# Where the remaining modulation sums are taken: first attention or merging stages

## The chip, the cores and the metric

One core of a Trainium2 chip. The metric is the time of one execution on the device in microseconds; a kernel is told by the median of its runs. Engines are named as the profile names them: PE is TensorE's matmul, PEld its weight load, DVE is VectorE, ACT ScalarE, POOL GpSimd and SP SyncE, which issues all the loads and stores of this kernel from one queue.

## What is computed

A backbone of two layers over 1024 latent tokens and 256 context tokens of 1024 channels. Each layer normalises its input and modulates it, runs three mixers beside each other (differential attention, a long convolution, a gated mixing of chunks), gates and projects each of them, merges the three by sigmoid gates, projects the result and adds it, gated, to its input. The modulation is a small product of a conditioning vector with a large matrix:

```python
def modulation(cond, w, b):
    m = jax.nn.silu(cond) @ w + b
    return jnp.split(m, 3, axis=-1)
...
        sh, sc, gt = modulation(c, ada_w[l], ada_b[l])
        shc, scc, gtc = modulation(c_ctx, ada_w[l], ada_b[l])
        h = rms_norm(x, norm_pre[l]) * (1.0 + sc[:, None]) + sh[:, None]
        hc = rms_norm(xc, norm_pre[l]) * (1.0 + scc) + shc
...
        x_new = x + gt[:, None] * rms_norm(out, norm_post[l])
```

There are two conditioning vectors, one for the latents (c) and one for the context (c_ctx), and the matrix of a layer has 1024 rows and 3072 columns, 24 blocks of 128.

## The kernel before, in words

Activations lie with 128 channels on the partitions and the tokens along the free dimension, in three chunks of 512, 512 and 256 tokens (the last is the context; layer 1 has only the first two in most places). Every dense product is three matmuls, on a rounded part (hh, wh) and what rounding left (hl, wl): mm3, lines 180 to 185. Weights come in blocks of 128 output channels through class Weights: SP loads a raw block wr (line 85, two buffers), ACT makes wh (line 103) and POOL, at some blocks DVE, makes wl (line 104), each with two buffers.

Stages follow each other: a first one with the filters and layer 0's first modulation part, and then in each layer phase_a (attention by heads, with blocks of the input projection as fill between its steps), phase_b (convolution and chunk mixing, with fill of the same kind), phase_m (merging) and phase_o or phase_last (output projection, with layer 0's also making layer 1's input).

The modulation has three uses in time. Layer 0's shift and scale (part 0) are needed at the very start and are made by matmuls (ada, line 247). Layer 0's gate (part 1) is needed in phase_o(0), layer 1's shift and scale at the end of phase_o(0), layer 1's gate in phase_last. These three are made by ada_rest (lines 275 to 297) on DVE: SP loads a piece aw of 128 rows by 256 of the 1024 columns of the transposed matrix (line 290, two buffers) and a piece acs of 256 columns of the two conditioning vectors, alike on every partition (line 286, one buffer, from csd); DVE multiplies them and sums over the columns with accum_out (line 293), once for each vector (for layer 1's gate once in all); four pieces make a row's sum, which a reduction joins (line 296). One step of this generator is one load of aw and its products. There are 32 steps for layer 0's gate, 64 for layer 1's shift and scale, and 32 for layer 1's gate. The scratch result at shares its two buffers (tag r2) with the rotary embedding of kvq (line 395), of which each head uses some before its sums.

In phase_a(0) the generator is laid beside the fill: after every second step of the fill one step of the sums (beside, line 157, used at line 570), and what is left after the four heads is drained (line 573). A head of layer 0 has 4 or 5 fill blocks of 12 steps.

phase_m (lines 1142 to 1189) goes over the three branches in the order 0, 2, 1. For each it loads the branch's output gy and its gate gg (lines 1159 and 1160), multiplies them (DVE and POOL by turns), and splits them into gh and gl. Then come 8 blocks of output channels: the sigmoid gates sel of the next block (gates, line 1195: computed from the input projection, evacuated by ACT at line 1201, or, if they were computed in an earlier stage, loaded and passed through ACT at lines 1208 and 1209), and the product pb of this block, multiplied by sel (line 1178 or 1180) and added into acc (line 1182, mostly POOL). In layer 0 the early gates are those of channels 2 to 7 of branches 2 and 1; branch 0's are all computed here. In branch 1 the sum is split at once into hh and hl for phase_o (line 1189).

The order on the engines is not simply that of the program's text. Tiles, buffers and semaphores are the framework's (TileContext): when the kernel is built, it lays out, engine by engine, the order in which instructions are handed to the queues; text that comes earlier has priority, and an instruction whose operands and buffer are reckoned to be there may go ahead of earlier text that has to wait. On the chip each engine takes its queue in that order.

Of the kernel before, what the change touches and what calls it, by code (L numbers as in the profile page):

```python
# [9 lines left out]
F32 = mybir.dt.float32  # L10
# [45 lines left out]
class Weights:  # L56
    """128-column blocks of weights in their order of use: loads and splits run ahead."""
# [13 lines left out]
    def again(self, i):  # L71
        """Whether use i is of the same block as the last but one use."""
        a, b = self.order[i - 2], self.order[i]
        return i > 1 and a[0] == b[0] == "out" and (a[1], a[3]) == (b[1], b[3])
# [65 lines left out]
def whole(x):  # L140
    """Block k of x [128, blocks, n], as pieces (columns, their source)."""
    return lambda k: [(slice(0, x.shape[2]), x[:, k, :])]
# [14 lines left out]
def beside(main, side):  # L157
    """main, with a step of side for every other step of it."""
    for i, w in enumerate(main):
        yield w  # L160
        if i % 2:
            next(side, None)


# [5 lines left out]
class Kernel:  # L170
# [16 lines left out]
    def rsqrt(self, out, x, t):  # L187
        """out = x ** -0.5 for x > 0, by Newton's steps from a guess of the exponent's bits."""
# [13 lines left out]
    def mean_rsqrt_steps(self, pool, psum, ss, n, width, tag="P"):  # L202
        """[128, n] of rsqrt(mean + eps), alike on every partition, from the [128, n] squares summed but
        for the sum over the partitions: the sums come as columns, the roots go out as rows."""
# [21 lines left out]
    def block(self, key, chunks, psum, evac, ahead=True):  # L226
        """One block of 128 output channels over the chunks of tokens; yields the weight of each step."""
# [19 lines left out]
    def ada(self, pool, psum):  # L247
        """Shift and scale of layer 0's modulation: rows of 256 channels, turned into columns."""
# [26 lines left out]
    def ada_rest(self, pool):  # L275
        """The other parts of the modulation, by sums over the free dimension."""
        nc = self.nc
        for l, part in ((0, 1), (1, 0), (1, 1)):
            b0, n = ((0, 16), (16, 8))[part]
            js = (0, 1) if (l, part) != (DEPTH - 1, 1) else (0,)  # L280
            sums = pool.tile([128, 16, 2, 4], F32, name="ams", tag="ams")
            ps = pool.tile([128, 16, 2], F32, name="amt", tag="amt")
            for i in range(4):
                s = slice(256 * i, 256 * i + 256)
                cs = pool.tile([128, 2, 256], F32, name="acs", tag="acs")
                nc.sync.dma_start(out=cs, in_=self.csd[:, :, s])
                for b in range(n):
                    w = pool.tile([128, 256], F32, name="aw", tag="aw", bufs=2)
                    t = pool.tile([128, 512], F32, name="at", tag="r2", bufs=2)[:, 0:256]
                    nc.sync.dma_start(out=w, in_=self.A["ada_wT"][l, b0 + b, :, s])  # L290
                    yield
                    for j in js:
                        nc.vector.scalar_tensor_tensor(out=t, in0=w, scalar=1.0, in1=cs[:, j, :], op0=MUL, op1=MUL,  # L293
                                                       accum_out=sums[:, b, j, i:i + 1])
            for j in range(2):
                nc.vector.reduce_sum(out=ps[:, 0:n, j], in_=sums[:, 0:n, j if j in js else 0, :], axis=AX.X)
            self.modulation(l, part, ps)
# [34 lines left out]
    def hnorm_steps(self, l, c, xt, r, pool, tag=None):  # L332
        """Normalised, modulated input of layer l for chunk c, split for the products."""
# [22 lines left out]
    def hmod(self, l, c, x):  # L356
        """As hnorm_steps, from the normalised input x [128, KT, n], in place."""
# [191 lines left out]
    def phase_a(self, l):  # L549
        nc = self.nc  # L550
        with ExitStack() as st:
# [8 lines left out]
            rest = self.ada_rest(P) if l == 0 else iter(())  # L560
            for h in range(HEADS):
# [8 lines left out]
                fill = beside(fill, rest)  # L570
                interleave(self.attn(l, h, P, psum), fill, 0.6 if l == 0 else 0.8)
                drain(fill)
            drain(rest)

# [1 line left out]
    # A sequence of 8 blocks of 128 is transformed at 2048 points: frequency p + 16 m comes from  # L576
    # A_p = sum_b u_b cos(pi p b / 8) and B_p = sum_b u_b sin(pi p b / 8), p = 0..8, through 128 x 128
    # matrices. Pair p holds (real | minus imaginary) of its 128 frequencies; p = 0 and p = 8 share one pair,
    # whose row 0 is (frequency 0 | frequency 1024), both real. Pairs 5, 6, 7 take -B_p and hold plus imaginary.
# [4 lines left out]
    def filter_hidden(self, l, P, psum):  # L584
        """Hidden features of the filters, [64, tokens], rounded over what rounding left; the context's apart."""
# [55 lines left out]
    def butterfly(self, U, P, ZW, pool_share):  # L641
        """U: [128, 10, w] with block b in slot SLOT[b]; yields a group's [(A, B), (A, B)]."""
# [52 lines left out]
    def transform(self, ps, p, pool, ra, rb, ia, ib):  # L695
        """Pair p into ps [128, 2, w]."""
# [9 lines left out]
    def back(self, ps, p, pool, y):  # L706
        """Pair p of products y [128, 2, 128] back to (A | B), [channels, 256]."""
# [1029 lines left out]
```

## Time and profile before

| | |
|---|---|
| median of 3 runs | 3242.26 us (3238.61 to 3243.84) |
| profiled execution, span from its first to its last instruction | 3238.8 us |
| profiled execution, own time | the page gives none beside the span |
| instructions | 43600 |
| TensorE's mean granted clock | 0.977 |

The median lies 3.5 us above the span of the profiled execution. A page of the profile is one execution: busy times of the engines, the span in slices, the transfers, the chain that ended last, and groups of instructions by line of the kernel. A group's line names the line of the kernel, the engine, the operation, what is written and read, the shapes and the count, then the busy time in us with the mean of one in ns, and the idle time of the engine just before such instructions with what ended most of it. Times within the span are counted from its start.

### The profile page before, as it was taken

The numbers are of one execution on the slowest core, as the hardware profiler recorded it, in microseconds if no ns is written. First come the engines' busy times: TensorE is split into PE (matmuls) and PEld (weight loads), VectorE is DVE, ScalarE is ACT, GpSimd is POOL, SyncE is SP. The second block draws the span as 40 slices with busy tenths as digits, with TensorE's granted clock in tenths as the row PEclk, the third lists the DMA queues.
The fourth block names the chain that finished last, engine by engine and source line by source line (L and its number), as shares of the span: only waits on it lengthen the run. The fifth ranks groups of instructions, "written<-read, shape, count | busy, mean of one in ns | idle before, by whom it ended". The sixth has DMA issues, their size and how long they took to land. (4 is left out here: it accounts for less than half of the span.)

```text
span 3238.8 us, 43600 instructions
## 1 busy us (share of the span) xinstructions
PE 3014.6 (93%) x16220; PEld 2529.3 (78%) x16220; DVE 1807.2 (56%) x3822; ACT 1219.6 (38%) x2015; POOL 958.5 (30%) x640
## 2 busy tenths in 40 slices
PE   8898999999989889999999899999998888899998
PEld 4687878788878777788877778888886767778878
DVE  6754767676875756202356745546456677432343
ACT  4322535353532423212344444545454233222231
POOL 1442020202023333212543322121214554321441
PEclk9899999999999999999999999999999999999999
DMA  6323222222356655413442421221214556542342
GB/s 240 111 85 107 76 72 77 78 76 77 109 187 200 196 162 184 142 40 99 130 159 86 156 64 49 66 60 60 62 61 156 188 178 192 169 156 80 112 134 79
DMA packets 234740, 381.62 MB, mean 118 GB/s; under 512 B 22622, under 2 KB 125406, under 8 KB 233248
## 3 DMA queue, kind: packets, MB, share of 16 engines
q1 hardware_dynamic: 234528, 378.83, 36.4%
q8 instruction: 128, 2.10, 0.3%
q14 instruction: 84, 0.69, 0.1%
HBM read 278.74 MB, written 90.57 MB: 114 GB/s over the span
## 5 line engine op out<-in xcount | busy, mean ns | idle before, releaser
L183 PE MATMUL pd<-hh,wh 128*128 128x512 f32 (+1 forms) x2784 | 1051.1, 378 | 11.0 <-DVE r L397 6.2
L185 PE MATMUL pd<-hh,wl 128*128 128x512 f32 (+1 forms) x2784 | 1037.4, 373 | 2.1 <-POOL wl L104 2.1
L184 PE MATMUL pd<-hl,wh 128*128 128x512 f32 (+1 forms) x2784 | 1038.1, 373 | 0.4 <-DVE hl L350 0.2
L104 POOL TENSOR_TENSOR wl<-wr,wh 128x1024 fp32r<-128x1024 f32 (+1 forms) x177 | 413.1, 2334 | 1416.3 <-ACT wh L103 1302.0
L183 PEld LDWEIGHTS pd<-hh,wh 128*128 128x128 f32 x2784 | 532.6, 191 | 93.0 <-DVE r L397 6.9
L185 PEld LDWEIGHTS pd<-hh,wl 128*128 128x128 f32 x2784 | 531.9, 191 | 87.0 <-POOL wl L104 2.5
L184 PEld LDWEIGHTS pd<-hl,wh 128*128 128x128 f32 x2784 | 532.6, 191 | 79.2 <-DVE hl L350 1.2
L103 ACT ACTIVATE wh<-wr 128x1024 fp32r<-128x1024 f32 (+1 forms) x204 | 194.9, 956 | 288.2 <-PE pd L184 135.4
L463 ACT ACTIVATE e<-S,sm 128x1280 f32<-128x1280 f32 (+1 forms) x144 | 177.7, 1234 | 203.9 <-DVE sm L461 184.8
L460 DVE TENSOR_REDUCE sm<-S 128x1 f32<-128x1280 f32 (+1 forms) x144 | 197.2, 1369 | 72.0 <-PE S L456 71.3
L183 PE MATMUL pb<-gh,wh 128*128 128x512 f32 (+1 forms) x480 | 178.4, 372 | 8.4 <-ACT gh L199 7.0
L185 PE MATMUL pb<-gh,wl 128*128 128x512 f32 (+1 forms) x480 | 178.3, 371 | 5.0 <-POOL wl L104 3.4
L184 PE MATMUL pb<-gl,wh 128*128 128x512 f32 (+1 forms) x480 | 178.5, 372 | 2.9 <-DVE gl L200 2.8
L456 PE MATMUL S<-K,q 128*128 128x512 f32 (+1 forms) x400 | 149.2, 373 | 13.9 <-ACT e L463 13.8
L293 DVE SCALAR_TENSOR_TENSOR at<-aw,acs 128x256 f32<-128x256 f32 x224 | 115.2, 538 | 47.3 <-DMA aw<-in_ada_wT 40.8
L456 PE MATMUL S<-K,w 128*128 128x512 f32 (+1 forms) x400 | 136.1, 354 | 0.0
L1178 DVE TENSOR_TENSOR acc<-pb,sel 128x512 f32<-128x512 f32 (+1 forms) x40 | 25.4, 637 | 189.7 <-PE pb L185 189.6
L200 DVE TENSOR_TENSOR pl<-T,ph 128x512 fp32r<-128x512 f32 x164 | 109.5, 686 | 33.2 <-ACT ph L199 31.6
L199 ACT ACTIVATE ph<-T 128x512 fp32r<-128x512 f32 x164 | 94.4, 596 | 73.7 <-PE T L493 73.6
L1182 POOL TENSOR_TENSOR acc<-acc,sel 128x512 f32<-128x512 f32 (+1 forms) x70 | 86.6, 1250 | 84.7 <-DVE sel L1180 84.6
L183 PEld LDWEIGHTS pb<-gh,wh 128*128 128x128 f32 x480 | 90.7, 189 | 26.8 <-ACT gh L199 8.6
L472 DVE SCALAR_TENSOR_TENSOR e<-e,sm,e 128x1280 f32<-128x1280 f32 (+1 forms) x72 | 104.7, 1455 | 10.5 <-ACT e L471 10.0
(405 smaller groups left out, 5228.0 us busy)
## 6 DMA issues: line engine op xcount, KB each, us to landing
wr<-in_w_in SPq DMA_DIRECT2D x136, 512.0 KB, 3.4
fm<-in_fmat SPq DMA_DIRECT2D x99, 192.0 KB, 3.1
fm<-in_imat SPq DMA_DIRECT2D x72, 256.0 KB, 3.0
aw<-in_ada_wT SPq DMA_DIRECT2D x128, 128.0 KB, 2.5
wr<-in_w_out SPq DMA_DIRECT2D x28, 512.0 KB, 3.4
zd<-zz SPq DMA_DIRECT2D x48, 256.0 KB, 2.0
z<-zd SPq DMA_DIRECT2D x24, 512.0 KB, 4.8
gd<-ev SPq DMA_DIRECT2D x48, 256.0 KB, 2.4
```

Source lines behind the costliest of these rows:

```text
L103: nc.scalar.activation(out=hi[:, 0:k, :], in_=t[:, 0:k, :], func=AF.Copy)
L104: eng.tensor_tensor(out=lo[:, 0:k, :], in0=t[:, 0:k, :], in1=hi[:, 0:k, :].bitcast(F32), op=SUB)
L183: mm(out, lhsT=wh, rhs=xh, start=first, stop=False)
L184: mm(out, lhsT=wh, rhs=xl, start=False, stop=False)
L185: mm(out, lhsT=wl, rhs=xh, start=False, stop=last)
L199: nc.scalar.activation(out=hi, in_=src, func=AF.Copy)
L200: nc.vector.tensor_tensor(out=lo, in0=src, in1=hi.bitcast(F32), op=SUB)
L293: nc.vector.scalar_tensor_tensor(out=t, in0=w, scalar=1.0, in1=cs[:, j, :], op0=MUL, op1=MUL, accum_out=sums[:, b, j, i:i + 1])
L456: nc.tensor.matmul(S[:, a - k0:b - k0], lhsT=st[:, o + 128 * t:o + 128 * t + 128], rhs=K[m][:, a:b], start=i == 0, stop=i == 1)
L460: nc.vector.reduce_max(out=sm[:, 0:1], in_=S[:, 0:nk], axis=AX.X)
L463: nc.scalar.activation(out=e[:, 0:nk], in_=S[:, 0:nk], func=AF.Exp, bias=sm[:, 1:2], scale=0.125, accum_out=sm[:, 2:3])
L472: nc.vector.scalar_tensor_tensor(out=e0[:, 0:nk], in0=e0[:, 0:nk], scalar=s0[:, 3:4], in1=e[:, 0:nk], op0=MUL, op1=ADD)
```

## The change

ada_rest takes the parts and the width of a piece as arguments. Layer 0's gate and layer 1's shift and scale are now summed in phase_m(0), in pieces of 128 columns; layer 1's gate in phase_m(1), in pieces of 256. The rows are taken in groups of 8 blocks, so that the partial sums are a smaller tile, and at gets a tag of its own with one buffer. In phase_m 9 steps in layer 0, and 2 in layer 1, follow each of the 24 blocks of products, and what is left is drained at the stage's end. beside and its use are gone. Steps: 64 + 128 in phase_m(0), 32 in phase_m(1). (Comments, which the change takes out too, are left out here.)

```diff
-def beside(main, side):
-    for i, w in enumerate(main):
-        yield w
-        if i % 2:
-            next(side, None)
...
-    def ada_rest(self, pool):
-        nc = self.nc
-        for l, part in ((0, 1), (1, 0), (1, 1)):
+    def ada_rest(self, pool, parts, w):
+        nc = self.nc
+        m = D // w
+        for l, part in parts:
             b0, n = ((0, 16), (16, 8))[part]
             js = (0, 1) if (l, part) != (DEPTH - 1, 1) else (0,)
-            sums = pool.tile([128, 16, 2, 4], F32, name="ams", tag="ams")
-            ps = pool.tile([128, 16, 2], F32, name="amt", tag="amt")
-            for i in range(4):
-                s = slice(256 * i, 256 * i + 256)
-                cs = pool.tile([128, 2, 256], F32, name="acs", tag="acs")
-                nc.sync.dma_start(out=cs, in_=self.csd[:, :, s])
-                for b in range(n):
-                    w = pool.tile([128, 256], F32, name="aw", tag="aw", bufs=2)
-                    t = pool.tile([128, 512], F32, name="at", tag="r2", bufs=2)[:, 0:256]
-                    nc.sync.dma_start(out=w, in_=self.A["ada_wT"][l, b0 + b, :, s])
-                    yield
-                    for j in js:
-                        nc.vector.scalar_tensor_tensor(out=t, in0=w, scalar=1.0, in1=cs[:, j, :], op0=MUL, op1=MUL,
-                                                       accum_out=sums[:, b, j, i:i + 1])
-            for j in range(2):
-                nc.vector.reduce_sum(out=ps[:, 0:n, j], in_=sums[:, 0:n, j if j in js else 0, :], axis=AX.X)
+            ps = pool.tile([128, n, 2], F32, name="amt", tag="amt")
+            for g in range(0, n, 8):
+                sums = pool.tile([128, 8, 2, m], F32, name="ams", tag="ams")
+                for i in range(m):
+                    s = slice(w * i, w * i + w)
+                    cs = pool.tile([128, 2, w], F32, name="acs", tag="acs")
+                    nc.sync.dma_start(out=cs, in_=self.csd[:, :, s])
+                    for b in range(8):
+                        a = pool.tile([128, w], F32, name="aw", tag="aw", bufs=2)
+                        t = pool.tile([128, w], F32, name="at", tag="at", bufs=1)
+                        nc.sync.dma_start(out=a, in_=self.A["ada_wT"][l, b0 + g + b, :, s])
+                        yield
+                        for j in js:
+                            nc.vector.scalar_tensor_tensor(out=t, in0=a, scalar=1.0, in1=cs[:, j, :], op0=MUL, op1=MUL,
+                                                           accum_out=sums[:, b, j, i:i + 1])
+                for j in range(2):
+                    nc.vector.reduce_sum(out=ps[:, g:g + 8, j], in_=sums[:, :, j if j in js else 0, :], axis=AX.X)
             self.modulation(l, part, ps)
...
-            rest = self.ada_rest(P) if l == 0 else iter(())
...
-                fill = beside(fill, rest)
                 interleave(self.attn(l, h, P, psum), fill, 0.6 if l == 0 else 0.8)
                 drain(fill)
-            drain(rest)
...
             ys = (self.ya[l], self.yd[l], self.yc[l])
+            rest = self.ada_rest(P, ((0, 1), (1, 0)), 128) if l == 0 else self.ada_rest(P, ((1, 1),), 256)
+            per = 9 if l == 0 else 2
...
                         if c == 0:
                             self.ws.ahead()
+                    for _ in range(per):
+                        next(rest, None)
                     if i == 1:
                         if d == 0:
                             self.mT = {c: self.alloc_h(c) for c in self.chunks(l)}
                         for c in self.chunks(l):
                             self.split(self.mT[c][0][:, d, :], self.mT[c][1][:, d, :], acc[c][:, d, :])
+            drain(rest)
```

## Rows read from the trace of the kernel before

**Rows 1.** The page, busy us of each engine over the span.

```profile
PE 3014.6 (93%) x16220; PEld 2529.3 (78%) x16220; DVE 1807.2 (56%) x3822; ACT 1219.6 (38%) x2015; POOL 958.5 (30%) x640
```

**Rows 2.** Stretches: length, busy us (PE, PEld, DVE, ACT, POOL), PEclk, DMA share, GB/s.

```profile
255.00:915.00 660.00, 626.58 (x3594) 535.06 (x3593) 446.12 (x1206) 297.33 (x481) 111.77 (x61) 0.99 0.27 85
1900.00:2400.00 500.00, 497.65 (x2691) 416.35 (x2690) 274.39 (x558) 247.45 (x367) 100.02 (x51) 1.00 0.18 59
1330.00:1676.00 346.00, 334.49 (x1717) 283.81 (x1716) 110.36 (x150) 91.62 (x166) 124.31 (x95) 0.99 0.35 106
2853.00:3126.00 273.00, 266.29 (x1151) 216.91 (x1150) 90.88 (x116) 74.46 (x118) 86.04 (x52) 0.99 0.36 114
```

**Rows 3.** The page's groups, the products of the sums.

```profile
L293 DVE SCALAR_TENSOR_TENSOR at<-aw,acs 128x256 f32<-128x256 f32 x224 | 115.2, 538 | 47.3 <-DMA aw<-in_ada_wT 40.8
```

**Rows 4.** Line 290, the loads of aw: issue on SP in ns, who waited, landing.

```profile
L290 SPq DMA_DIRECT2D aw<-in_ada_wT x128: 327/333/1944, 268.3 to 916.4; - x128
...
  DVE at L293: 40.8, 31
...
DMA to landing us min/median/max: 2.3/2.5/7.9
```

**Rows 5.** Stretches: the four bursts of sums within the first attention (columns as rows 2).

```profile
290.00:366.00 76.00, 70.86 (x384) 60.52 (x384) 53.35 (x153) 32.39 (x49) 12.18 (x7) 0.96 0.35 109
466.00:535.00 69.00, 62.52 (x348) 52.69 (x347) 50.63 (x150) 30.69 (x46) 7.39 (x3) 0.98 0.34 103
625.00:690.00 65.00, 61.80 (x352) 52.16 (x351) 49.39 (x150) 30.64 (x46) 7.38 (x3) 1.00 0.35 110
775.00:921.00 146.00, 138.22 (x805) 117.32 (x804) 109.76 (x333) 70.01 (x113) 17.36 (x8) 1.00 0.36 113
```

**Rows 6.** Waits of PE in 255 to 915 us: total, times, longest.

```profile
PE S L456 <- ACT e L463: 13.8, 5, 4.5
PE mrb L218 <- DVE mn L195: 9.9, 5, 2.2
```

**Rows 7.** Timeline of DVE, a product of 128 columns (start us, us, engine, line).

```profile
932.52 1.12 DVE L1109 SCALAR_TENSOR_TENSOR bs<-mm,cols,bs 128x128 f32<-128x128 f32 x4
```

**Rows 8.** Timeline of DVE, end of the first attention, line 293.

```profile
911.66 0.42 DVE L293 SCALAR_TENSOR_TENSOR at<-aw,acs 128x256 f32<-128x256 f32 x1
912.00 0.08 DVE L293 DVE_READ_ACCUMULATOR at<-aw,acs 128x1 f32 x1
...
912.92 0.43 DVE L293 SCALAR_TENSOR_TENSOR at<-aw,acs 128x256 f32<-128x256 f32 x1 [0.84 <-DMA aw<-in_ada_wT]
...
914.99 0.43 DVE L293 SCALAR_TENSOR_TENSOR at<-aw,acs 128x256 f32<-128x256 f32 x1 [1.64 <-DMA aw<-in_ada_wT]
...
918.00 0.43 DVE L293 SCALAR_TENSOR_TENSOR at<-aw,acs 128x256 f32<-128x256 f32 x1 [1.81 <-DMA aw<-in_ada_wT]
```

**Rows 9.** Timelines of PE and ACT at the start of the first merging stage.

```profile
1336.43 0.28 PE L183 MATMUL pd<-hh,wh 128*128 128x256 f32 x1
...
1339.88 0.58 ACT L1201 ACTIVATE sel<-pd 128x512 f32<-128x512 f32 x1
...
1350.21 0.28 PE L183 MATMUL pd<-hh,wh 128*128 128x256 f32 x1
...
1358.15 0.58 ACT L1201 ACTIVATE sel<-pd 128x512 f32<-128x512 f32 x1
```

**Rows 10.** Timeline of one block of branch 2 in the first merging stage.

```profile
1541.90 0.33 SPq L85 DMA_DIRECT2D wr<-in_w_br  x1
1543.15 2.26 SPq L1208 DMA_DIRECT2D sel<-sd  x3
...
1546.72 0.62 ACT L103 ACTIVATE wh<-wr 128x512 fp32r<-128x512 f32 x1
...
1547.47 1.30 POOL L104 TENSOR_TENSOR wl<-wr,wh 128x512 fp32r<-128x512 f32 x1 [2.41 <-issue]
...
1548.50 0.40 PE L183 MATMUL pb<-gh,wh 128*128 128x512 f32 x1
```

## The prediction

> **What bounds the kernel now.** I read the page's busy shares first, then the table of stretches, TensorE's waits, and last the timelines of the two places that the change touches. TensorE is busy 3014.6 of 3238.8 us, so a change gains only where TensorE idles and costs only where it makes TensorE idle [rows 1]. The stretches show that this holds in both places. In the first attention (255 to 915 us) TensorE is busy 626.6 of 660 us and VectorE 446; in the second (1900 to 2400), which has no such sums (and more filling work per step, 0.8 against 0.6), TensorE idles 2.4 us in 500. In the first merging stage (1330 to 1676) TensorE is busy 334.5 of 346 us while VectorE works only 110 [rows 2]. So the sums leave a stage where VectorE is pressed and go to one where it has room. The question is what they bring along: a load for each step, on SP's one queue.
>
> **What leaves the first attention.** 224 products of 256 columns, each with its accumulator read, 115.2 us of VectorE [rows 3], 128 loads and 12 of csd on SP, and 40.8 us in which VectorE stood before a piece that had not landed [rows 4]. The sums come in four bursts, one for each head, the last with the rest. TensorE's idle time in these bursts is 76 - 70.9, 69 - 62.5, 65 - 61.8 and 146 - 138.2 us, together 22.6 us [rows 5], of 33.4 in the whole attention. What TensorE waits for is the score tile S, free after exp, which waits for VectorE's maximum (13.8 us), and the root of the norm (9.9 us) [rows 6]. The second is a chain of small operations at the heads' ends, mostly outside the bursts; it stays. The gain is therefore between 0 and 22.6 us. I take 12, about half: a head's first score has little beside it with or without the sums, and what is late next is that same wait on exp. The 115 us of VectorE time are not the gain, since TensorE covers all but these 22.6.
>
> **What arrives, as work.** Layer 0's stage gets 64 + 128 = 192 steps of 128 columns, each a load of 64 KB and two products, and 24 loads of csd. A product of 128 columns takes 0.28 us (1.12 for four) [rows 7]; with the 0.08 of an accumulator read [rows 8] two make 0.72 us, so 138 us in all. VectorE would be at 110 + 138 = 248 of 346 us: no bound. SP issues 216 loads of 0.33 us [rows 4], 71 us in 346: no bound either. Layer 1's stage gets 32 steps of one 256-column product (0.50 us, 16 us in all) and 4 loads of csd, beside 90.9 us of VectorE in 273 (2853 to 3126). The reductions and the final modulation are the same few operations as before: nothing. The scratch tile at has its own buffer and is written by VectorE alone: nothing. In layer 1 I put the whole at nothing, hidden under the gate products of the first branch; if that cover is gone, it costs the lateness worked out below, 32 steps of it, 10 us.
>
> **What arrives, as a chain.** The pieces have two buffers, so a load waits for the products two steps earlier and they wait for the load. The end of the attention shows this chain in the open: products at 911.66, 914.99 and 918.00 are two steps apart, 3.2 us for two steps with one product each [rows 8], which is the landing of 2.5 us [rows 4] and 0.5 us of work and some handing over. With 0.72 us of work I take 3.3 us for two steps: 192 steps make 317 us. csd has one buffer, so each of its 24 loads puts about 2.5 - 0.8 = 1.7 us of extra wait into the chain (0.84 is what a step waits anyway [rows 8]): 41 us. The chain is 358 us long, in a stage of 346 us. It can begin as soon as the stage's buffers are there, since the framework puts on each queue what it reckons to be ready: the bursts show it, 24 loads within some 65 us, far ahead of the fill that the program hands them out by.
>
> The Trainium skill (DMA: Bandwidth & Descriptors, "Anatomy of one DMA" and "Rules for kernel authors") speaks against narrow pieces: a transfer pays some 2.0 us whatever its size, and under 64 KB one pays mostly overhead. By its formula, given for GpSimd's path, 64 KB would land in 2.15 us, an estimate that would shorten the chain by 192 x 0.35 / 2 = 34 us against my 2.5. No row here shows a 64 KB piece.
>
> **Why a chain beside a full TensorE can cost.** Each engine works off its queue in the order that the framework fixed when the kernel was built. If a chain is slower on the chip than the framework reckoned, what stands behind it on the queue comes late although it could go. The start of this very stage shows it. The gate products of chunk 1 end when those of chunk 2 begin, at 1336.43, and ACT takes them at 1339.88; one block on they end at 1350.21 and ACT takes them at 1358.15, each time behind copies of gh, that hang on a chain of loads with two buffers [rows 9]. TensorE went 13.8 us ahead, the chain 18.3: it is a third slower than planned, and lateness grew from 3.4 to 7.9 us.
>
> What stands behind the pieces on SP is the weights wr, the stored gates sel and the branch inputs. In branches 2 and 1, whose gates mostly are stored already, there is no room: wr is issued at 1541.90 and sel at 1543.15, ACT copies wh at 1546.72 and POOL makes wl from 1547.47 to 1548.77, while the block that needs it starts at 1548.50 [rows 10]. With a landing like aw's 2.5 us, wr lies there some 2 us before its copy. In branch 0 there is more room, but lateness is carried on. On VectorE the products stand before pb's evacuation; PSUM's 7 tiles cover that for over 10 us, and I cost it at nothing; without that cover it would add a step's wait to each of the later blocks.
>
> **The price of the lateness.** Below: 0, if the framework reckons these loads rightly (a gain is excluded, TensorE being the bound there). Above: 4.5 of every 18.3 us of the 358, so 88 us, if the chain is as much slower than planned as in [rows 9]. Between them lie the rows of the same loads in the attention: VectorE waited 40.8 us for 128 loads, 0.32 us a load [rows 4], though other work stood between. I take that, being of the same kind of load: 192 x 0.32 = 61 us, less 4 us of room ahead of the weights, 57 us. **Sum:** -12 + 57 + 0 = +45 us. The profiled execution has a span of 3238.8 us and no other time shown; the median is 3.5 us above it. On the median: 3242.3 + 45 = 3287 us.
>
> **Rivals.** First, **faster**: the framework's pace is right, or jitter is taken up by the room ahead of the weights. Then the sums disappear into VectorE's idle 236 us and only the 12 us of the attention count (5 to 20): 3230 us. It decides where the lateness stays under some 0.08 us a step (16 us in 192). For it: VectorE at 110 of 346 us and the 2.4 us of idle TensorE in the second attention. Against it: [rows 9] and the 40.8 us. The Trainium skill (Perfetto Trace Analysis, "Optimization Strategy") would side with it: stages with different limits may be interleaved for a gain. Chance 0.22.
> Second, **much slower**: the chain is late by the full 88 us, and runs past the end of the stage (1330 + 358 = 1688 against 1676), so that it is late to the last. With no gain in the attention: 3242 + 88 - 4 = 3326 us. For it: [rows 9]; against it: that chain also has ACT and POOL in it. Chance 0.15.
> Third, **nothing to see**: gain and loss cancel, or neither exists, since the scores wait with or without the sums. 3242 us, chance 0.13.
> The forecast has 0.50, its own range from 20 to 68 us slower: 3262 to 3310 us.
>
> **How the numbers follow.** 0.2%, 6.5 us, is about what a measurement can tell here. Faster is the first rival, 0.22; same the third, 0.13; slower the forecast and the second, 0.65. The range takes in the first rival down to 3228 us and the second up to 3330; what lies outside is about 0.10 of their tails.
>
> **What would show it.** Right: L293's line in 384 + 32 products, most with a wait for aw, starting about 1318 us (the stage comes 12 us earlier) and running through the merging stage; the stage longer than 346 us by some 57; TensorE's new waits there on wl, wh and gh; no score wait of over 3 us in the first attention. Wrong: TensorE in the merging stage as busy as before with the sums between its blocks (then the first rival), or the stage longer with waits of TensorE on VectorE's own results (then VectorE's queue, which I cost at nothing, is what decides), or the sums outside the stage.

## The result, and the profile after

The changed kernel took 3273.5 us (median of 4 runs, 3269.9 to 3276.0) against 3243.1 for the kernel before (4 runs, 3238.6 to 3249.0): a ratio of 1.0097, 95% interval 1.0085 to 1.0109. It is slower by 30 us by the medians and by 31 by the ratio; the forecast was slower by 45. The profiled execution has a span of 3274.2 us, 35.4 over that of before. Where it went is read best from first and last matmuls of the stages: the first attention's last score starts at 868.1 us instead of 896.5, the merging stage's first branch product (pb) at 1327.5 instead of 1353.1, the first output product (po) at 1705.3 instead of 1674.4, the last one of layer 0 at 1850.8 instead of 1815.9. From there on the two kernels stay 35 us apart to the end. So the attention gave 28 us (some 3 of them were lost again before the merging stage), the merging stage took 56, the output stage 4, layer 1 nothing. The output stage (first to last po of layer 0) is between 141 and 148 us long over all the traces, and 143.7 in the run without any sums, so its 4 us are not clear of that spread.

The stretches of the changed kernel, with the columns of [rows 2]: the attention; the merging stage from before its first pb (as long a run-in as in [rows 2]); its three branches apart; layer 1's merging stage. Each fence below is one answer.

```profile
255.00:887.00 632.00, 618.79 (x3577) 528.16 (x3576) 342.57 (x755) 294.24 (x479) 110.89 (x61) 0.99 0.18 58
```

```profile
1304.00:1707.00 403.00, 355.50 (x1716) 296.16 (x1716) 244.04 (x880) 92.08 (x166) 126.07 (x95) 0.93 0.44 128
2889.00:3162.00 273.00, 266.99 (x1156) 217.84 (x1155) 109.05 (x185) 74.93 (x119) 86.48 (x52) 0.99 0.42 134
```

```profile
1327.00:1518.00 191.00, 173.30 (x872) 147.20 (x871) 104.25 (x435) 31.87 (x53) 37.75 (x23) 0.95 0.35 106
1518.00:1622.00 104.00, 89.55 (x434) 74.10 (x433) 64.35 (x221) 24.88 (x46) 48.18 (x40) 0.93 0.53 154
1622.00:1705.00 83.00, 67.90 (x288) 53.51 (x286) 62.59 (x196) 28.13 (x54) 34.59 (x28) 0.86 0.44 124
sum 378.00, PE 330.76 PEld 274.81 DVE 231.20 ACT 84.88 POOL 120.52; mean PE 110.25 PEld 91.60 DVE 77.07 ACT 28.29 POOL 40.17
```

The same three branches in the kernel before:

```profile
1353.00:1528.00 175.00, 169.18 (x869) 144.25 (x868) 35.68 (x51) 34.60 (x60) 39.54 (x25) 0.98 0.25 78
1528.00:1611.00 83.00, 83.00 (x434) 71.13 (x433) 29.46 (x40) 23.36 (x44) 47.87 (x39) 1.00 0.48 141
1611.00:1674.00 63.00, 57.68 (x288) 47.06 (x286) 34.39 (x49) 26.49 (x51) 31.73 (x27) 1.00 0.37 112
sum 321.00, PE 309.86 PEld 262.44 DVE 99.53 ACT 84.44 POOL 119.14; mean PE 103.29 PEld 87.48 DVE 33.18 ACT 28.15 POOL 39.71
```

The stage's 57 us have two parts. TensorE's idle time went from 321 - 309.9 = 11 to 378 - 330.8 = 47 us, 36 more. And about the same matmuls (1594 records, 1591 before) were busy 21 us longer, at a granted clock of 0.95, 0.93 and 0.86 where it had been 0.98, 1.00 and 1.00. Busy time times granted clock comes to 306 us in both kernels, so the clock accounts for the 21 us. One idle stretch shows how: TensorE stands from 1526.1 to 1532.9 us, and in the 4 us after it the granted clock is 0.50, the lower of its two levels (1.2 instead of 2.4 GHz), before it rises again.

```profile
1518.00:1525.50 7.50, 7.45 (x37) 5.92 (x36) 4.48 (x21) 3.35 (x9) 1.73 (x2) 1.00 0.64 175
1525.50:1533.00 7.50, 0.66 (x3) 0.22 (x3) 3.59 (x15) 0.60 (x2) 2.53 (x2) 0.67 0.64 190
1533.00:1537.00 4.00, 4.00 (x10) 3.13 (x11) 0.83 (x7) 0.00 (x0) 0.00 (x0) 0.50 0.53 158
1537.00:1541.00 4.00, 4.00 (x18) 3.30 (x17) 2.98 (x16) 0.00 (x0) 1.36 (x2) 0.84 0.17 44
```

So each microsecond of waiting in the stage cost over half of one more (21 of 36). What TensorE waited for, from 1315 to 1710 us:

```profile
PE pb L177 <- POOL wl L104: 12.6, 10, 6.8
PE pd L177 <- POOL wl L104: 10.8, 2, 7.4
PE pb L175 <- ACT wh L103: 9.1, 3, 3.5
PE pb L175 <- ACT gh L191: 8.5, 4, 3.8
PE po L175 <- DVE sel L1173: 3.1, 1, 3.1
PE pd L175 <- DVE acc L1171: 2.3, 1, 2.3
```

Weights first (wl, wh), then the branch inputs (gh). GpSimd's wl operations in the stage took no longer than before (56.6 us, 56.9 before); they started late. The products themselves, L287 (L293 in [rows 3]), and their loads, L284 (L290 in [rows 4]), by source:

```profile
L287 DVE SCALAR_TENSOR_TENSOR at<-aw,acs x416: 273/292/2601, 1314.3 to 2971.5; 128x128 f32<-128x128 f32 x128, 128x256 f32<-128x256 f32 x11
...
  DMA aw<-in_ada_wT: 102.8, 99
  DMA acs<-csd: 47.2, 18
```

```profile
L284 SPq DMA_DIRECT2D aw<-in_ada_wT x224: 327/328/1517, 1306.8 to 2969.0; - x112
...
DMA to landing us min/median/max: 1.8/2.2/5.3
```

There are 384 + 32 products, from 1314 us on, and VectorE waited for 99 of the 224 loads. The 192 loads of 64 KB in layer 0's stage landed in 2.1 us in the median. In the attention TensorE's waits of [rows 6] shrank from 13.8 to 4.7 us (S on exp) and from 9.9 to 2.6 (the root).

### The profile page after: what moved, and what is told of

It is laid out like the page before. It is cut to its first block, busy times and chain, and to the rows that moved or that the text cites. A ratio compares the mean times of both kernels' runs of the same rounds, so it can differ in the third digit from the quotient of the medians.

```text
span 3274.2 us, 44381 instructions
## 1 busy us (share of the span) xinstructions
PE 3038.0 (93%) x16220; PEld 2547.1 (78%) x16220; DVE 1856.7 (57%) x4208; ACT 1216.9 (37%) x2015; POOL 958.7 (29%) x640
## 5 line engine op out<-in xcount | busy, mean ns | idle before, releaser
L287 DVE SCALAR_TENSOR_TENSOR at<-aw,acs 128x128 f32<-128x128 f32 (+1 forms) x416 | 184.7, 444 | 160.3 <-DMA aw<-in_ada_wT 102.8
L175 PE MATMUL pb<-gh,wh 128*128 128x512 f32 (+1 forms) x480 | 184.6, 385 | 20.2 <-ACT wh L103 10.2
L177 PEld LDWEIGHTS pb<-gh,wl 128*128 128x128 f32 x480 | 94.2, 196 | 36.7 <-POOL wl L104 18.3
L466 DVE SCALAR_TENSOR_TENSOR e<-e,sm,e 128x1280 f32<-128x1280 f32 (+1 forms) x72 | 111.6, 1549 | 10.0 <-ACT e L465 9.5
```

The costliest lines, as they stand in the source:

```text
L175: mm(out, lhsT=wh, rhs=xh, start=first, stop=False)
L177: mm(out, lhsT=wl, rhs=xh, start=False, stop=last)
L287: nc.vector.scalar_tensor_tensor(out=t, in0=a, scalar=1.0, in1=cs[:, j, :], op0=MUL, op1=MUL, accum_out=sums[:, b, j, i:i + 1])
L466: nc.vector.scalar_tensor_tensor(out=e0[:, 0:nk], in0=e0[:, 0:nk], scalar=s0[:, 3:4], in1=e[:, 0:nk], op0=MUL, op1=ADD)
```

## The experiments

The kernel before was run again beside each group of experiments, so each total stands as a ratio to the runs on its own chip; the stage (from the first pb to the first po of layer 0) is from the run's trace. SP's lead is the time within the stage for which SP stands at the weights' loads (L85) because their buffer is not free yet: as long as it has to wait there, it is early.

| kernel | us | ratio to before (95%) | stage, us | SP's lead, us |
|---|---|---|---|---|
| before | 3243.1 | 1 | 321.3 | 172 |
| changed | 3273.5 | 1.0097 (1.0085 to 1.0109) | 377.8 | 12 |
| no sums | 3209.2 | 0.9909 (0.9892 to 0.9925) | 320.4 | 171 |
| products, no loads | 3228.2 | 0.9973 (0.9962 to 0.9984) | 336.4 | 182 |
| loads, tiny products | 3253.3 | 1.0046 (1.0031 to 1.0061) | 362.6 | 10 |
| four buffers | 3263.3 | 1.0080 (1.0065 to 1.0095) | 369.5 | 37 |
| loads unread | 3232.6 | 0.9982 (0.9970 to 0.9993) | 336.2 | 71 |
| four buffers, 8 csd loads | 3248.4 | 1.0027 (1.0015 to 1.0040) | 351.6 | 48 |
| pairs, 8 csd loads | 3251.4 | 1.0039 (1.0028 to 1.0050) | 359.3 | 45 |
| loads on GpSimd's queue | 3334.5 | 1.0287 (1.0266 to 1.0309) | 416.7 | 136 |

My theory (A) was that of the prediction: the chain load, product, load with two buffers is slower than planned, and what stands behind it is late. Its rival (B) was VectorE's own work.

**No sums.** In ada_rest:

```diff
-            for g in range(0, n, 8):
...
-            self.modulation(l, part, ps)
+            nc.vector.memset(ps, 0.0)
+            for _ in range(8 * m * n // 8):
+                yield
+            self.modulation(l, part, ps)
```

> Leaves out all of the weighted sums (the parts are set to the bias alone): no loads, no products. Every theory expects the same here, the floor: the first attention as quick as in the changed kernel (28 us earlier than before), the merging stage of layer 0 back at some 321 to 326 us from its first branch product to the first output product (321.4 before, 377.8 after), so about 3215 us. If the stage stays over 340 us, the lateness has nothing to do with the sums.

As expected: 0.9909, 29 us under the kernel before, with the stage at 320.4. This is the floor. The changed kernel, 31 us over before, is 31 + 29 = 60 us over this floor, and that is what the sums cost it in the stage and behind it.

**Products without loads.**

```diff
+        a = pool.tile([128, w], F32, name="aw", tag="aw", bufs=1)
+        cs = pool.tile([128, 2, w], F32, name="acs", tag="acs")
+        nc.vector.memset(a, 1.0)
+        nc.vector.memset(cs, 1.0)
...
-                    nc.sync.dma_start(out=cs, in_=self.csd[:, :, s])
...
-                        nc.sync.dma_start(out=a, in_=self.A["ada_wT"][l, b0 + g + b, :, s])
```

> All products stay, on one constant piece that is never loaded (neither ada_wT nor csd is read, so the sums are others). Theory A (the chain of loads with two buffers makes what stands behind it in the queues late): the stage is back near 321 to 330 us, total 3215 to 3222 us. Theory B (VectorE's own work, 185 us of it, standing before the evacuations and the sel products): the stage stays at 365 us or more, total 3260 us or more. Between them, the difference to the run without sums is what VectorE's work costs.

Neither number: 0.9973 and a stage of 336.4 us, 16 over the floor. So VectorE's work alone costs 16 us of the changed kernel's 57, and taking the loads away gives back the other 41 (377.8 - 336.4). I had costed VectorE's queue at nothing.

**Loads with tiny products.**

```diff
-                            nc.vector.scalar_tensor_tensor(out=t, in0=a, scalar=1.0, in1=cs[:, j, :], op0=MUL, op1=MUL,
+                            nc.vector.scalar_tensor_tensor(out=t[:, 0:2], in0=a[:, 0:2], scalar=1.0, in1=cs[:, j, 0:2], op0=MUL, op1=MUL,
```

> All loads stay, in the same order and with the same two buffers, but each product takes 2 of the 128 (or 256) columns, so VectorE's work shrinks by more than half (the sums are others). Theory A: the stage stays long, 350 to 375 us, total 3245 to 3270 us. Theory B: the stage is near 321 to 335 us, total 3215 to 3230 us.

As A expected: stage 362.6, 42 over the floor, and TensorE waits for weights:

```profile
PE pb L177 <- POOL wl L104: 13.1, 10, 6.3
PE pb L175 <- ACT wh L103: 13.0, 5, 8.2
```

The 42 are not the share of the loads alone, though. VectorE's work shrank less than I had expected, from 168 + 31 to 107 + 31 us in the stage:

```profile
L287 DVE SCALAR_TENSOR_TENSOR at<-aw,acs 128x2 f32<-128x2 f32 x384 | 106.8, 278 | 146.5 <-DMA aw<-in_ada_wT 95.4 <-DMA acs<-csd 40.0 <-issue 1.8
L287 DVE DVE_READ_ACCUMULATOR at<-aw,acs 128x1 f32 x384 | 31.4, 82 | 0.2 <-issue 0.2
```

So loads 42 and products 16 add up to 58 of the changed kernel's 57, but that is no clean split; the 41 us of the run before are the better number for the loads.

**Four buffers.** Scratch and sums go to the PSUM bank that the stage does not use, which makes the room:

```diff
+            bank = psum.tile([128, 512], F32, name="bank", tag="T")
...
-                sums = pool.tile([128, 8, 2, m], F32, name="ams", tag="ams")
+                sums = bank[:, 0:16 * m].rearrange("p (b j i) -> p b j i", b=8, j=2)
...
-                        a = pool.tile([128, w], F32, name="aw", tag="aw", bufs=2)
-                        t = pool.tile([128, w], F32, name="at", tag="at", bufs=1)
+                        a = pool.tile([128, w], F32, name="aw", tag="aw", bufs=4 if w == 128 else 2)
+                        t = bank[:, 256:256 + w]
```

> Pieces get four buffers instead of two in layer 0's stage; to make room, the products' scratch and the sums lie in the PSUM bank that the stage has unused. Loads, products and csd's one buffer stay. Theory A: a load has twice the time, so most of the lateness goes: stage 325 to 345 us, total 3218 to 3238 us. Theory B (VectorE's work) and theory C (the count of loads on SP's queue): nothing changes, 3265 to 3280 us.

Theory A, as I had it, falls: VectorE now waits only 10.2 us for pieces around the stage instead of 74.5, and the stage is still 369.5 us.

```profile
DVE bank L287 <- DMA aw<-in_ada_wT: 10.2, 15, 1.6
```

Twice the depth gained 8. The wait had moved to SP's own queue. There, in the stage of the kernel before, SP had time to stand before weights whose buffer was not free yet; in the changed kernel it has not; with four buffers it has little. The waits of SP in the stage, before, changed and with four buffers:

```profile
SPq L85 <- POOL wl L104: 172.1, 32, 14.9
```

```profile
SPq L284 <- DVE at L287: 112.2, 110, 3.8
SPq L284 <- DMA aw<-in_ada_wT: 29.1, 35, 2.6
...
SPq L85 <- POOL wl L104: 11.6, 10, 2.5
```

```profile
SPq L284 <- DVE bank L287: 117.2, 124, 4.8
...
SPq L85 <- POOL wl L104: 37.2, 18, 6.4
```

L85 is the load of wr. Before, SP came to it 172 us too early in all: that was the weights' lead. In the changed kernel it stands 141 us before the loads of pieces, because the buffer's last product has not run or its last load not landed, and the lead is 12. More buffers take away its waits for landings (29 us), not those for products (112 and 117 us): the loads run further ahead of VectorE until SP again stands before a full buffer. That is theory A2. Theory C was the plain count of issues and the traffic.

**Loads unread**, all loads issued, the products on a constant piece (scratch and sums in the PSUM bank as with four buffers):

```diff
+        k = pool.tile([128, w], F32, name="ak", tag="ak", bufs=1)
+        nc.vector.memset(k, 1.0)
...
-                            nc.vector.scalar_tensor_tensor(out=t, in0=a, scalar=1.0, in1=cs[:, j, :], op0=MUL, op1=MUL,
+                            nc.vector.scalar_tensor_tensor(out=t, in0=k, scalar=1.0, in1=k, op0=MUL, op1=MUL,
```

> All 192 loads of pieces and 24 of csd are still issued on SP, but nothing reads them: the products (all of them) work on a constant piece, so the sums are others. A load now waits at most for the landing of an earlier load into its buffer (three buffers), never for a product; scratch and sums in the spare PSUM bank as in the run with four buffers. Theory A2 (SP stands, in order, before loads whose buffers the products still hold, and the weights' loads behind them come late): total near the run without loads, 3225 to 3238 us, and SP again waits over 100 us in the stage for a free wr buffer, as before the change. Theory C (the count of issues on SP, or the loads' traffic): near the run with four buffers, 3253 to 3268 us.

Total as A2 expected: stage 336.2, the same as without loads. So 216 issues and their 16 MB cost the stage nothing; what costs is that loads and products wait for each other. Of these waits, four buffers had left those of the loads for the products and VectorE's for csd (next). SP's lead came back less far than I had written, 71 us in the stage instead of over 100:

```profile
SPq L85 <- POOL wl L104: 71.0, 24, 6.7
```

**Fewer csd loads.** With one buffer, the 24 loads of csd held VectorE 38.1 us in the run with four buffers. Here the slice is the outer loop:

```diff
+        for i in range(m):
+            s = slice(w * i, w * i + w)
+            cs = pool.tile([128, 2, w], F32, name="acs", tag="acs")
+            nc.sync.dma_start(out=cs, in_=self.csd[:, :, s])
+            for r, (l, part, b) in enumerate(rows):
...
```

> As the run with four buffers, but csd is loaded 8 times instead of 24 in layer 0's stage (each slice serves all 24 blocks before the next). If VectorE's 38 us of waiting for csd, with its one buffer, is what was left there (theory D): 3232 to 3248 us. Theory A2: a gain of at most 5 to 10 us, since SP still stands before some 190 loads: 3253 to 3262 us. Theory C: 16 issues fewer of 216, under 3 us: 3260 to 3266 us.

1.0027: 17 us by the ratios under four buffers (0.0053 x 3240), at the edge of theory D's range and beyond A2's, so csd's single buffer was a cost of its own. Why it helps is in line with A2: VectorE stands less, so its buffers come free sooner, SP comes to the weights 47.7 us early in all, and the stage falls to 351.6.

```profile
SPq L282 <- DVE bank L285: 115.3, 139, 3.1
SPq L85 <- POOL wl L104: 47.7, 19, 5.4
```

**Pairs**, 128 KB for two blocks, so half the loads:

```diff
+                if r % 2 == 0:
+                    b += ((0, 16), (16, 8))[part][0]
+                    pair = pool.tile([128, 2, w], F32, name="aw", tag="aw", bufs=256 // w)
+                    nc.sync.dma_start(out=pair, in_=self.A["ada_wT"][l, b:b + 2, :, s].rearrange("b p c -> p b c"))
+                a = pair[:, r % 2, :]
```

> As the run with 8 csd loads, but one load brings two blocks' pieces (128 KB, two buffers): 96 loads instead of 192, the same products. Theory A2: half as many places where SP stands: 3235 to 3250 us. Theory C: 3240 to 3250 us too. Theory B (VectorE's work): no gain over the run before it in this list.

No gain: 1.0039 against 1.0027, with intervals that overlap. A2 and C had both expected some; only theory B, VectorE's work, had expected none. SP's standing before products did not halve with the loads, it was 118.7 us in 77 waits instead of 116.3 in 142 (1300 to 1720 us): its length does not follow the number of loads, and VectorE's pace is the reading that is left. The table bears A2 out in its own way. Less the 16 us of the products, the loads cost the stage 41 us at a lead of 12 (changed), 33 at 37 (four buffers), 23 at 45 (pairs), 15 at 48 (8 csd loads) and nothing at 71 (unread). That the two go together does not by itself prove which makes which.

**GpSimd's queue.**

```diff
-                        nc.sync.dma_start(out=a, in_=self.A["ada_wT"][l, b0 + g + b, :, s])
+                        nc.gpsimd.dma_start(out=a, in_=self.A["ada_wT"][l, b0 + g + b, :, s])
```

> The changed kernel, with the loads of pieces issued by GpSimd's queue instead of SP's (csd stays on SP); two buffers. Theory A2: SP's waits for a free wr buffer come back (over 100 us in the stage, 12 in the changed kernel) and TensorE's waits for wh go, but POOL now stands before the loads, so wl and POOL's sums of acc come late in their place: 3260 to 3300 us, with TensorE's waits on wl and acc. If it was the length of the load chain alone, whatever queue it is on, nothing changes: 3270 us and the same waits as in the changed kernel. If SP's issue time was it (theory C): 3228 to 3240 us.

A2's signs, at a higher price than I gave: 1.0287, stage 416.7. SP is early at the weights again (135.5 us from 1300 to 1720 us) and TensorE's wait for wh falls from 9.1 to 2.6, but now GpSimd stands before the loads, and what it makes itself, wl, is late:

```profile
PE pb L177 <- POOL wl L104: 35.0, 13, 9.0
PE pd L177 <- POOL wl L104: 20.7, 7, 4.5
```

The same loads, on another queue, make late what stands behind them there. How much of that is standing and how much the issuing itself (0.54 us of GpSimd's time a load, some 103 us in the stage) was not held apart.

**The attention.** Its gain was 28 us where my bound had been 22.6, so four runs asked what the sums had cost there. Theory V: VectorE's work. Theory L: the waits for pieces.

> The kernel before, with its sums in the first attention, but no piece and no csd is loaded: all 224 products work on a constant piece (the sums are others). It tells where the 28 us come from that the first attention gave. Theory V (VectorE's 115 us of products in a stage where the scores wait for VectorE's maximum): most of the 28 us stay, total 3230 to 3240 us. Theory L (the waits for pieces, on SP and VectorE): most go, 3210 to 3220 us.

```diff
+        w = pool.tile([128, 256], F32, name="aw", tag="aw", bufs=1)
+        cs = pool.tile([128, 2, 256], F32, name="acs", tag="acs")
+        nc.vector.memset(w, 1.0)
+        nc.vector.memset(cs, 1.0)
...
-                    nc.sync.dma_start(out=w, in_=self.A["ada_wT"][l, b0 + b, :, s])
```

Outside both ranges: 1.0046 (1.0028 to 1.0064), slower than with the loads. The products' line by source shows what changed: unpaced by loads they come in dense bursts. The first line is this run, the second the kernel before (busy tenths in 40 slices of the span):

```profile
busy tenths in 40 slices 0003030303200000000000000000000000000000
```

```profile
busy tenths in 40 slices 0001112112210000000000000000000000000000
```

TensorE waited 21.3 us for exp there instead of 13.8.

> The kernel before, all loads in their order, but each product takes 2 of 256 columns (the sums are others), so that VectorE's 115 us shrink to some 54. Theory V: about half of the 28 us go, total 3220 to 3228 us. Theory L: nearly all stay, 3232 to 3240 us.

```diff
-                        nc.vector.scalar_tensor_tensor(out=t, in0=w, scalar=1.0, in1=cs[:, j, :], op0=MUL, op1=MUL,
+                        nc.vector.scalar_tensor_tensor(out=t[:, 0:2], in0=w[:, 0:2], scalar=1.0, in1=cs[:, j, 0:2], op0=MUL, op1=MUL,
```

1.0003 (0.9986 to 1.0019): theory L's range. With half the products' time, nothing was gained: VectorE stood 54.1 us before pieces (40.8 in the kernel before), exp waited behind it, and TensorE's wait for exp was 21.0 us instead of 13.8. ACT's waits in the attention, this run and then the kernel before:

```profile
ACT e L463 <- DVE sm L461: 67.1, 40, 4.1
ACT e L463 <- DVE at L293: 56.1, 15, 6.0
```

```profile
ACT e L463 <- DVE sm L461: 102.0, 55, 5.5
```

ACT's total does not tell the loss by itself: in the changed kernel, with no sums there, exp still waits 109.3 us for the maximum.

The last part alone, (1, 1), to layer 1's stage:

```diff
-        for l, part in ((0, 1), (1, 0), (1, 1)):
+        for l, part in ((0, 1), (1, 0)):
...
+            rest = self.ada_late(P, ((1, 1),), 256) if l else iter(())
```

> The kernel before, with only the part (1, 1), a quarter of the loads and a seventh of the products, moved to layer 1's merging stage; the other two parts stay in the first attention. Layer 1's stage took them for nothing in the changed kernel. Theory L: a quarter of 28 us, 3230 to 3233 us; theory V: a seventh, 3233 to 3236 us. Both expect it under both kernels.

0.9991 (0.9977 to 1.0006): no difference that this measurement can tell, with a median (3237.9 us) above both ranges; the attention's last score came 3.8 us earlier in the trace. And neither loads nor long products:

> The kernel before, its sums in the first attention without loads and with products of 2 of 256 columns on a constant piece (the sums are others): neither waits for pieces nor long products, 224 products of 0.16 us and their accumulator reads, 54 us of VectorE. Without loads alone the kernel took 3253.7 us, with short products alone 3239.5, before 3237.9; without any sums 3209. Theory Q (VectorE's time in front of a score's maximum costs, be it spent on a product or in a wait for a piece, and each of the two runs kept one of them and bunched it more): 3212 to 3226 us. If the order in which the instructions were put costs by itself, whatever their length: 3235 us or more.

```diff
-                        nc.vector.scalar_tensor_tensor(out=t, in0=w, scalar=1.0, in1=cs[:, j, :], op0=MUL, op1=MUL,
+                        nc.vector.scalar_tensor_tensor(out=t[:, 0:2], in0=w[:, 0:2], scalar=1.0, in1=cs[:, j, 0:2], op0=MUL, op1=MUL,
```

(on top of the run without loads). 3211.8 us against 3230.4 for the kernel before on that chip, 0.9939 (0.9922 to 0.9955): 20 of the 29 us to be had by the ratios; by the trace the last score starts at 868.8 us, as in the run without any sums (869.4), and TensorE's wait for exp is as short as in the changed kernel (4.7):

```profile
PE S L456 <- ACT e L463: 4.6, 3, 1.5
```

By the ratio (3218 us where the kernel before takes 3237.9) this lies in theory Q's range, and Q is the reading that fits these runs: VectorE's time in front of a score's maximum costs, be it spent on a product or before a piece. Taking one away alone gained nothing; only without both does most of the cost go.

No kernel that computes everything came out under the kernel before by more than can be measured. The room is there (the floor is 29 us lower), but no run found a place for the sums in it.

## Why the prediction was right, and where its steps were not

**The sign and the size were right, for a reason named only in part.** The stage was to cost 57 us and cost 56.5; the whole 45, and it was 30 by the medians, 35 by the profiles.

*What leaves the attention: 12 us, between 0 and 22.6.* It was 28. The step that failed is the bound: I counted only TensorE's idle time inside the four bursts [rows 5]. The root's wait, of which I wrote "it stays", went from 9.9 to 2.6 us, and TensorE's busy time in the whole attention fell from 626.6 to 618.8 us for about the same matmuls. Idle time in the attention fell from 33.4 to 13.2 us: 20 of the 28 are idle time, 7 of these the root's wait that I had ruled out, and 8 are busy time, which I had not counted at all. The mean granted clock of the attention rose from 0.987 to 0.995, which makes some 5 of these 8; the window also has 17 fewer matmul records, some 3.

*The work.* 138 us for layer 0's products: it was 168 + 31 for the accumulator reads. My 0.28 us for a product came from rows in which GpSimd did nothing [rows 7]; see below.

*The chain.* The pace was right in branch 0, where 8 steps took some 15 us as worked out (3.3 us for two, and csd), but in the later branches they took 15 to 22. So the loads ran from 1307 to 1725 us, past the end of the stage: 418 us where I had 358. csd's single buffer was worth naming: it held VectorE 41 us there, as worked out, and with four buffers taking 16 of its 24 loads away gained 17.

*The price, 0.32 us a load.* The size was near (57), the mechanism half of it. I took the price from VectorE's waits for pieces, as if the landing was what came late. Four buffers took those waits away and gained 8 us. The runs put in its place: SP, in order, stands before a load until VectorE has left its buffer, and the weights' lead of 172 us shrinks to 12 (the loads bring 41 of the 57 us, by the run without them); and VectorE's work alone, which I costed at nothing under the cover of PSUM's 7 tiles, costs 16. My 57 for the loads alone was too much by about what I had left out for VectorE. That PE waits on wl, wh and gh was right. How it goes is seen at one place of the changed kernel, the second block of branch 2. SP, behind pieces and csd, issues a load of the next branch's input, gy from yd, at 1526.89 and its gate gg at 1527.83:

```profile
1525.07 0.37 SPq L284 DMA_DIRECT2D aw<-in_ada_wT  x1
1525.67 0.52 SPq L280 DMA_DIRECT2D acs<-csd  x1
1526.29 0.55 SPq L284 DMA_DIRECT2D aw<-in_ada_wT  x1
1526.89 0.43 SPq L1152 DMA_DIRECT2D gy<-yd  x1
1527.83 0.33 SPq L1153 DMA_DIRECT2D gg<-gd  x1
```

In GpSimd's queue the product of this gy stands ahead of the block's wl, in both kernels. GpSimd waits for the load and only then makes wl, whose wh had been ready at 1526.1, and TensorE stands 6.84 us. In the kernel before SP issued the same load 0.4 us after branch 2's first product (1528.04 against 1527.66), here 9.2 us after it (1517.73):

```profile
1530.35 1.26 POOL L1154 TENSOR_TENSOR gy<-gy,gg 128x512 f32<-128x512 f32 x1 [6.50 <-DMA gy<-yd]
1531.57 1.31 POOL L104 TENSOR_TENSOR wl<-wr,wh 128x512 fp32r<-128x512 f32 x1
```

```profile
1532.94 0.79 PE L177 MATMUL pb<-gh,wl 128*128 128x512 f32 x1 [6.84 <-POOL wl L104]
```

*Layer 1: nothing.* Right: TensorE is busy 267.0 of 273 us where it was 266.3 [rows 2], with 18 us more on VectorE.

*Not in the sum:* the lower granted clock behind the idle stretches, 21 of the 57 us. My price, being taken from VectorE's waits, held no clock. That the stage came within a microsecond is therefore luck: a price for the wrong wait, too high for the loads, met a cost of VectorE's work and of the clock that I had not counted. Whether the chain, which ran on into the output stage, cost the 4 us there is open, since runs without it are as long there.

*The rivals.* The first (the sums disappear in VectorE's idle time) fails on SP's queue; the loads unread show that without the waits it would have been nearly right, at 3233 us. The second was right that the chain outlasts the stage, but its 88 us did not come; the third (no difference) lies outside the interval. The rule of the Trainium skill that I weighed against my 2.5 us for a landing (DMA: Bandwidth & Descriptors, "Anatomy of one DMA") gave 2.15 us for 64 KB, an estimate. The trace agrees, with 2.1 us in the median of the 192 loads of that size on SP's queue; on GpSimd's, for which the rule is given, the run above has 2.4. So on SP the rule was the better number, but the landing was not what decided.

## What to carry to other kernels

A load is not only a transfer: on an in-order queue it is a place where the issuing engine stands until the buffer's last reader is done. Ask what stands behind it, and read the lead there (how long the queue waits for a free buffer at the loads that matter, summed over the stage) before adding to that queue; more buffers for the added loads gave back only 25 of the lost 160 us of lead here. An engine that idles much of its time is room only if its queue has nothing urgent behind the filling work, and a stage bound by a full TensorE can give back more than TensorE's idle time in the places where the filler visibly runs, as the attention did here (28 us against 22.6).

## What the runs showed that I had not expected

VectorE's products stretch under GpSimd. Over the trace of the changed kernel, the 384 products of 128 columns in and around layer 0's stage took 0.29 us in the mean where no GpSimd operation overlapped them (297) and 0.93 us where one did (87). One of them, in the timelines of GpSimd and VectorE:

```profile
1443.85 2.39 POOL L104 TENSOR_TENSOR wl<-wr,wh 128x1024 fp32r<-128x1024 f32 x1 [12.92 <-ACT wh L103]
1443.95 2.44 DVE L287 SCALAR_TENSOR_TENSOR at<-aw,acs 128x128 f32<-128x128 f32 x1 [2.08 <-DMA acs<-csd]
```

It starts 0.1 us after wl and ends 0.15 us after it. The products of the branches with sel, of which one input is PSUM, show no such thing: of those with 512 columns, 0.68 us with an overlap (5) and 0.68 without (27). The Trainium skill (SBUF — State Buffer, "SBUF: two separate sides") says that GpSimd and a VectorE operation with two SBUF inputs take a shared port pair by turns, for a whole instruction; both rows agree. It was in the trace of before as well, where gl (two SBUF inputs), with 512 columns, took 1.46 us with an overlap (17) and 0.69 without (6). The 87 products lost some 56 us of VectorE so, which nearly explains the 199 us in place of 138. The tiny products show it too: 0.85 us in the mean with an overlap (66), 0.16 without (318), which is why they freed so little of VectorE. Whether the 16 us that products without loads cost come from this was not tried.

Also, GpSimd's queue was dearer than SP's: an issue took 0.54 us there (0.33 on SP), GpSimd stood 201 us in the whole run until VectorE had left a piece's buffer, and layer 1's merging stage, which the changed kernel leaves as it was (261.8 us from first pb to first po, 262.7 before), took 286.2 us.
